# Stick-breaking attention: the last key's values are added in branch A's staging on GpSimd instead of in the eviction

## The chip, the cores and the metric

One core of a Trainium2 chip runs the whole layer. The metric is the device time of one execution in microseconds. TensorE (PE) multiplies, VectorE (DVE) and ScalarE (ACT) work on tiles in SBUF and read TensorE's results from PSUM banks, GpSimd (POOL) works on SBUF alone, SyncE (SP) issues most DMAs. Each engine runs its own instructions in a fixed order and waits for others on semaphores.

## The reference

One layer of an encoder, 1024 tokens by 1024 channels, in float32. The part that matters here is attention and the projection behind it:

```python
for i in range(s_len // Q_BLOCK):                      # 8 blocks of 128 queries
    z = jnp.einsum('bhqd,bhkd->bhqk', qb, kp) * inv_sqrt
    mask = s_idx < t_idx
    log_not = jnp.where(mask, jax.nn.log_sigmoid(-z), 0.0)
    excl = lax.cumsum(log_not, axis=3, reverse=True) - log_not
    a = jnp.where(mask, jnp.exp(jax.nn.log_sigmoid(z) + excl), 0.0)
    outs.append(jnp.einsum('bhqk,bhkd->bhqd', a, vp))
...
y_b = cb * causal_dwconv(cc * cx, conv_w[l])
merged = (jax.nn.sigmoid(ga) * (y_a @ w_branch_a[l])
          + jax.nn.sigmoid(gb) * (y_b @ w_branch_b[l]))
```

There are 16 heads of 64 channels. Behind this follow an output projection, a residual sum and a SwiGLU feed-forward part.

## The kernel before

Every matrix product is done in three passes of rounded parts: a float32 operand is split into a high part (a copy on ACT) and a low part (a subtraction on DVE), and high x high, high x low and low x high are summed in PSUM.

**Attention's arithmetic.** The weights of a row of keys are differences of running products, so the kernel sums the running products against differences of neighbouring value rows, and adds one value row by itself: that of the last key that a block of 128 queries can see. These rows, turned so that channels lie on partitions, are the small tile `vlast`; before it is 64 channels x 16 heads x 8 blocks. `load_vlast` loads them in two halves of 8 heads, and `turn_vlast` turns them on PE with small transposes and copies them out.

**Steps.** `attention` is a generator that goes through 128 steps (16 heads x 8 query blocks i). A step issues the scores of its block (`att_scores`: matmuls into a bank `z`, a sigmoid on ACT into `pt`, a triangular mask on POOL, line 927), then the transposes of the block two steps back (`att_trans`: PE into a bank `tr`, split into the tiles `ath`/`atl` or `afh`/`afl` by ACT and DVE, lines 952 to 958), then its own running product (`att_scan`: a scan on DVE, line 937, and the odd columns on POOL, which appears under the helper's line 133 as `pt<-pt`). Bank `z` has two buffers, and five tiles `pt` go round.

**Values.** `att_av` multiplies four blocks of one head (g = 0 or 1: queries 0 to 511 or 512 to 1023) into the bank `o`, of which there is one. Partitions 0 to 63 and 64 to 127 of `o` hold two partial sums. The eviction follows: ACT copies the lower half to `oy` in four pieces of 128 columns, each with its block's column of `vlast` as a bias (line 975), DVE adds the upper half (line 977), and SP stores `oy` to `d_ya` (line 978). `att_av` yields after every second key block, and `attention` takes so many of these pieces at each step as its two small tables say. The next group cannot begin in `o` before DVE's addition has read it.

**Fillers.** Between attention's matmuls PE works on independent matmuls into the banks `pj`: the B section with the convolution, then branch B's projection (lines 1033 to 1035). Branch A's projection runs behind attention, and its first products stand already among the last fillers.

**Branch A's staging** (lines 1182 to 1188). For 16 pieces (two halves n of the tokens, eight pairs k of heads) SP loads `yr` from `d_ya`, ACT copies the high part and DVE subtracts for the low one, into tiles `ya` that take over attention's buffers. `yr` uses the four buffers of `ybh` and `ybl`, so a load waits for the split of the piece four before it. The first loads come before attention has ended, as soon as the buffers are free.

**Order.** Matmuls keep the order in which the code is written, and so do attention's instructions on DVE and POOL (lines 1131 to 1137). All else is placed by a scheduler that simulates the engines' timeline; what it decides is fixed when the program is built.

Of the kernel before, what the change touches and what calls it, by code (L numbers as in the profile page):

```python
# [9 lines left out]
F32 = mybir.dt.float32  # L10
F32R = mybir.dt.float32r
AF = mybir.ActivationFunctionType
ALU = mybir.AluOpType
# [4 lines left out]
P = 128  # L18
T = 1024
D = 1024  # L20
KT = D // P
H = 16
DH = 64
# [7 lines left out]
def block_kernel(tc, x, x_t, cols, ada_1, ada_2, ada_row, w_q, w_kv, w_cg, w_a, w_b, w_o, w_g, w_u, w_d, out):  # L31
    nc = tc.nc
# [7 lines left out]
    def nm(s):  # L40
        uid[0] += 1
        return f"{s}_{uid[0]}"
# [42 lines left out]
    ident = const.tile([P, P], F32, name="dm")  # L85
# [46 lines left out]
    def tt(eng, out, a, b, op):  # L132
        eng.tensor_tensor(out=out, in0=a, in1=b, op=op)  # L133
# [195 lines left out]
    for whole in (1, 1, 0, 0, 1, 1, 0, 1, 1, 1, 1):  # L329
        for e in range(2 - whole):  # L330
            r = slice(0, P) if whole else slice(64 * e, 64 * e + 64)
# [495 lines left out]
    bp = s3.enter_context(tc.tile_pool(name="phb", bufs=1, reuse_waits="tile"))  # L827
# [6 lines left out]
    def att_load(h):  # L834
        pr, e0 = h // 2, (h % 2) * DH
        sqt = bp.tile([P, T], F32R, tag="sq", bufs=2, name=nm("sqt"))
        skh = bp.tile([P, T], F32R, tag="skh", bufs=2, name=nm("skh"))
        skl = bp.tile([P, T], F32R, tag="skl", bufs=2, name=nm("skl"))
        for e in range(2):
            es = slice(e * DH, (e + 1) * DH)  # L840
            nc.sync.dma_start(sqt[es].bitcast(F32), d_q[e][pr, e0:e0 + DH, :])
            nc.sync.dma_start(skh[es].rearrange("p (i t) -> p i t", t=P).bitcast(F32), d_k[0][pr // 4][:, e0:e0 + DH, pr % 4].rearrange("i p t -> p i t"))
            nc.sync.dma_start(skl[es].rearrange("p (i t) -> p i t", t=P).bitcast(F32), d_k[1][pr // 4][:, e0:e0 + DH, pr % 4].rearrange("i p t -> p i t"))
        hd[h] = (sqt, skh, skl)

    def load_v(h, e):

        pr = h // 2
        d = d_v[h // 8][pr % 4]
        t_ = ("vb", "va")[e]  # L850
        vab[t_] = first_va if (h, e) == (0, 1) else v_tile(e)
        lastld[0] = nc.sync.dma_start(vab[t_], d[e:P + e])

    def att_dv(h, part):

        va, vb = vab["va"], vab["vb"]
        cs = slice(h % 2 * DH, h % 2 * DH + DH)
        dv = vb[:, :, cs]
        if part == 0:
            tt(nc.vector, dv, dv, va[:, :, cs], ALU.subtract)  # L860
            return
        vt = vts[h] = bp.tile([P, KT, P], F32R, tag="vt", bufs=2, name=nm("vt"))
        nc.scalar.activation(vt[:, :, :DH], dv, AF.Copy)
        tt(nc.vector, vt[:, :, DH:], dv, vt[:, :, :DH].bitcast(F32), ALU.subtract)

    def load_vlast(e):

        vl = bp.tile([9 - e, 512], F32, tag="vl", bufs=1, name=nm("vl")) if e else first_vl
        nc.sync.dma_start(vl[:8].rearrange("i (r d) -> i r d", d=P), d_v[e][:, P].rearrange("r i d -> i r d"))
        if e == 0:  # L870
            nc.sync.dma_start(vl[8:9], d_b)
        return vl

    def turn_vlast(e, vl):
        tr = pps.tile([P, 512], F32, tag="tr", bufs=NTR, name=nm("tr"))
        n = 9 - e
        for h in range(8):
            nc.tensor.transpose(tr[:DH, h * n:h * n + n], vl[:, h * DH:(h + 1) * DH], ident[:n, :n])
        o, t = vlast[:, 8 * e:8 * e + 8], tr[:DH, :8 * n].rearrange("p (h i) -> p h i", i=n)
        if e:  # L880
            nc.scalar.activation(o, t, AF.Copy)
        else:
            nc.scalar.activation(o, t[:, :, :8], AF.Copy)
            nc.vector.tensor_tensor(out=o, in0=o, in1=t[:, :, 8:9].broadcast_to([DH, 8, 8]), op=ALU.add)

    vlast = bp.tile([DH, H, 8], F32, name="vlast")
    hd, vts, vab = {}, {}, {}

    def at_tile(full):
# [43 lines left out]
    def att_scan(h, i):  # L933
        pt, off = ptof[h, i], D - (i + 1) * P
        first = pt[:, slice(D - 1, off, -2)]
        both = pt[:, slice(D - 2, off - 1 if off else None, -2)]
        nc.vector.tensor_tensor_scan(out=both, data0=first, data1=both, initial=1.0, op0=ALU.mult, op1=ALU.mult)  # L937
        mid = pt[:, slice(off + 1, D - 2, 2)]
        tt(nc.gpsimd, mid, mid, pt[:, slice(off + 2, D - 1, 2)], ALU.mult)
# [21 lines left out]
    def att_av(h, g):  # L961
        pr, e0 = h // 2, (h % 2) * DH
        vt = vts[h]
        o = pps.tile([P, 512], F32, tag="o", bufs=1, name=nm("o"))
        for j in range(4 * g + 4):
            full, d = j < 4 * g, j % 4
            c0 = 0 if full else d * P
            for e, t in enumerate(ats[h, g, full]):
                lastav[0] = nc.tensor.matmul(o[:, c0:], vt[:, j, :], t[:, 4 * d * P:4 * d * P + 512 - c0],  # L969
                                             start=(j + e == 0), stop=(j == 4 * g + 3 and e == 1))  # L970
            if j % 2 and j < 4 * g + 3:
                yield 0
        yv = bp.tile([DH, 512], F32, tag="oy", bufs=2, name=nm("oy"))
        for e in range(4):
            nc.scalar.activation(yv[:, e * P:(e + 1) * P], o[:DH, e * P:(e + 1) * P], AF.Identity,
                                 bias=vlast[:, h, 4 * g + e:4 * g + e + 1])
        nc.vector.tensor_tensor(out=yv, in0=o[DH:], in1=yv, op=ALU.add)
        nc.sync.dma_start(d_ya[g][e0:e0 + DH, pr, :], yv)
        yield 0
# [5 lines left out]
    def attention():  # L985

        av = []
        steps = [(h, i) for h in range(H) for i in (LAST if h == H - 1 else ORDER)]
        for s in range(len(steps) + DAV):
            flush[0] = s >= len(steps)  # L990
            if s < len(steps):
                h, i = steps[s]
                if s % 8 == (0 if h else 3) and h + 1 < H:
                    with tc.issue_after(lastld[0].ins):
                        att_load(h + 1)
                with tc.issue_after(lastz[0].ins) if s else ExitStack():
                    if s in (1, 2):
                        att_dv(0, s - 1)
                    if s % 8 in ((4, 6) if h % 2 else (3, 5)) and h + 1 < H:
                        att_dv(h + 1, s % 8 // 5)  # L1000
                    if s % 16 in (6, 7) and s + 16 < len(steps):
                        load_v(2 * (s // 16) + 2, 7 - s % 16)
                if s == 54:
                    with tc.issue_after(lastld[0].ins):
                        vl = load_vlast(1)
                if s == 56:
                    turn_vlast(1, vl)
                yield from att_scores(h, i)
            tr_ = att_trans(*steps[s - 2]) if 0 <= s - 2 < len(steps) else iter(())
            if s >= DAV and steps[s - DAV][1] % 4 == 3:  # L1010
                av[:] = [att_av(steps[s - DAV][0], steps[s - DAV][1] // 4)]
            yield from itertools.islice(tr_, 1)
            if s < len(steps):
                yield from (a_ for q in av[:1] for a_ in itertools.islice(q, (0, 0, 0, 0, 1, 0, 1, 0)[s % 8]))
            yield from tr_
            if s < len(steps):
                att_scan(*steps[s])
            for q in av[:1]:
                yield from itertools.islice(q, 9 if s >= len(steps) else (2, 0, 2, 0, 2, 0, 2 * (s > 8 * H - 8), 0)[s % 8])

    def ps_f():
        return pps.tile([P, 512], F32, tag="pj", bufs=NPJ, name=nm("pj"))
# [80 lines left out]
    with tc.high_priority():  # L1103
        att_load(0)
        for j in range(HEAD):
            next(fl)
            if j == 1:
                vl = load_vlast(0)
# [3 lines left out]
                for e in range(2):  # L1112
                    nc.sync.dma_start((hh, hl)[e][1][:, :4].bitcast(F32), d_h[e])
    at_ = attention()
    flush, nfl = [0], 0
    pe, mine = len(nc.cur_bb.bb.instructions), set()
# [64 lines left out]
    with tc.high_priority():  # L1181
        for j, (ya2, (n, k)) in enumerate(zip(ya_slots(), [(0, k) for k in range(7)] + [(1, 0), (1, 1), (1, 2), (0, 7)] + [(1, k) for k in range(3, 8)])):
            yr = fq.tile([P, 512], F32, tag=("ybh", "ybl")[j % 2], bufs=2, name=nm("yr"))
            nc.sync.dma_start(yr, d_ya[n][:, k, :])
            h_, l_ = ya2[:, 0], ya2[:, 1]
            nc.scalar.activation(h_, yr, AF.Copy)
            tt(nc.vector, l_, yr, h_.bitcast(F32), ALU.subtract)
            yah[n][k], yal[n][k] = h_, l_
# [141 lines left out]
    for ch in range(2):  # L1330
# [21 lines left out]
        for i in (0, 4, 1, 2, 3, 5, 6, 7) if ch else range(8):  # L1352
            n, t0 = i // 4, (i % 4) * P
# [37 lines left out]
            r = rstd_of(ss, 1.0 / D, dp, 1)  # L1391
# [412 lines left out]
```

## Time and profile before

| | |
|---|---|
| median of 3 runs | 1794.71 us (1792.99 to 1795.57) |
| profiled execution | 1793.84 us, of which the span 1791.8 us |
| granted TensorE clock | 1.00 in the whole span |
| PE busy | 1780.3 us, 99% of the span |
| ACT, DVE, POOL busy | 826.5, 1271.2, 342.1 us |
| attention | from about 597 us to 983 us of the span |
| branch A's staging, loads | first issue at 778.2 us, last at 986.0 us |

PE is the engine that sets the time. Matmuls are pipelined, so a matmul's length in the trace overlaps the next one's; time that PE loses shows in the distance between the starts of two of them. A 512-column matmul is followed by the next after 0.23 us.

### The profile page before, as it was taken

The page shows a single profiled execution, that of the slowest core. Times are in us where ns is not written, and L with a number is a line of the kernel's source. Part 1 is how long each engine was busy: PE and PEld are TensorE (multiplying, and loading weights), DVE is VectorE, ACT ScalarE, POOL GpSimd, SP SyncE. Part 2 cuts the span into 40 slices and gives each one's busy share as a digit, 9 for nine tenths or more (in the row PEclk, how much of TensorE's full clock was granted, in tenths as well). Part 3 has the DMA queues.
Part 4 walks back from the last instruction along what each step waited for, and adds up shares of the span by engine and source line. Part 5 has one row for each costly group of instructions (what it writes and reads, how often), then busy time and mean ns, then how long its engine had stood idle before and what let it go on. Part 6 is the DMA issues. An engine that isn't in the chain of part 4 may idle for free.

```text
span 1791.8 us, 24274 instructions
## 1 busy us (share of the span) xinstructions
PE 1780.3 (99%) x8355; PEld 1469.9 (82%) x8355; DVE 1271.2 (71%) x1998; ACT 826.5 (46%) x1555; POOL 342.1 (19%) x437
## 2 busy tenths in 40 slices
PE   9999999999999999999999999999999999999999
PEld 6888877888888788888888888888888888888887
DVE  6876487777874678777786764698867777643866
ACT  5534364333433567666675221764544444432320
POOL 0024334734231233333342100100000000000000
PEclk9999999999999999999999999999999999999999
DMA  9579655222634977797654866425534344399776
GB/s 375 168 244 384 238 190 165 76 92 93 230 133 147 295 190 200 209 326 196 162 140 167 286 210 208 129 95 170 207 130 149 145 186 158 138 343 331 262 232 219
DMA packets 162447, 359.05 MB, mean 200 GB/s; under 512 B 15026, under 2 KB 56330, under 8 KB 161172
## 3 DMA queue, kind: packets, MB, share of 16 engines
q1 hardware_dynamic: 125740, 289.65, 49.2%
q10 hardware_dynamic: 33096, 55.25, 8.7%
q0 software_dynamic: 3488, 12.59, 2.0%
q8 instruction: 67, 1.10, 0.2%
q14 instruction: 56, 0.46, 0.1%
HBM read 247.84 MB, written 109.62 MB: 200 GB/s over the span
## 4 chain that ended last, share of the span: by engine, by line
PE 91%; DMA 4%; DVE 2%; ACT 1%; issue 1%; POOL 1%; SPq 0%; POOLq 0%; DVEq 0%; ACTq 0%
PE e L128 8%; PE e L129 8%; PE e L127 8%; PE pj L127 7%; PE pj L128 7%; PE pj L129 7%; PE pj L294 7%; PE pj L1033 4%; PE pj L1035 4%; PE pj L1034 4%; PE o L969 3%; PE e L1631 3%; PE e L1633 3%; PE e L1632 3%; PE tr L952 3%; PE z L922 2%
## 5 line engine op out<-in xcount | busy, mean ns | idle before, releaser
L1247 ACT ACTIVATE whi<-raw 128x512 fp32r<-128x512 f32 x137 | 84.9, 628 | 159.4 <-PE e L128 101.9
L1248 DVE TENSOR_TENSOR wlo<-raw,whi 128x512 fp32r<-128x512 f32 x137 | 93.0, 686 | 67.6 <-ACT whi L1247 50.1
L133 POOL TENSOR_TENSOR pt<-pt 128x63 f32<-128x63 f32 (+7 forms) x128 | 97.8, 764 | 211.0 <-DVE pt L937 198.2
L128 PE MATMUL e<-big,whi 128*128 128x512 f32 x352 | 136.9, 389 | 0.0
L127 PE MATMUL e<-big,whi 128*128 128x512 f32 x352 | 136.5, 390 | 0.0
L129 PE MATMUL e<-big,wlo 128*128 128x512 f32 x352 | 136.1, 389 | 0.0
L294 PE MATMUL pj<-whi,big 128*128 128x512 f32 x448 | 132.9, 393 | 0.8 <-ACT big L263 0.5
L133 DVE TENSOR_TENSOR c<-pj,c 128x512 f32<-128x512 f32 x140 | 93.5, 683 | 52.9 <-PE pj L129 52.3
L924 ACT ACTIVATE pt<-z,rq 128x128 f32<-128x128 f32 (+1 forms) x192 | 107.3, 580 | 48.0 <-PE z L923 41.8
L127 PE MATMUL pj<-big,whi 128*128 128x512 f32 x320 | 124.9, 390 | 0.0
L129 PE MATMUL pj<-big,wlo 128*128 128x512 f32 x320 | 124.7, 390 | 0.0
L128 PE MATMUL pj<-big,whi 128*128 128x512 f32 x320 | 124.6, 389 | 0.0
L1632 PE MATMUL e<-wlo,f 128*128 128x512 f32 (+1 forms) x319 | 121.8, 382 | 0.0
L1631 PE MATMUL e<-whi,f 128*128 128x512 f32 (+1 forms) x319 | 121.6, 382 | 0.0
L1633 PE MATMUL e<-whi,f 128*128 128x512 f32 (+1 forms) x319 | 121.6, 382 | 0.0
L133 DVE TENSOR_TENSOR wlo<-raw,whi 128x512 fp32r<-128x512 f32 x108 | 91.6, 852 | 34.6 <-ACT whi L524 34.5
L524 ACT ACTIVATE whi<-raw 128x512 fp32r<-128x512 f32 x108 | 67.4, 630 | 99.6 <-PE pj L128 49.8
L1033 PE MATMUL pj<-big,whi 128*128 128x512 f32 x256 | 112.8, 440 | 0.0
L127 PE MATMUL e<-rh,whi 128*128 128x512 f32 x264 | 102.7, 389 | 0.0
L128 PE MATMUL e<-rl,whi 128*128 128x512 f32 x264 | 102.7, 389 | 0.0
L129 PE MATMUL e<-rh,wlo 128*128 128x512 f32 x264 | 102.0, 389 | 0.0
L937 DVE TENSOR_TENSOR_SCAN pt<-pt 128x64 f32<-128x64 f32 (+7 forms) x128 | 95.9, 749 | 8.2 <-POOL pt L927 7.6
(348 smaller groups left out, 4678.2 us busy)
## 6 DMA issues: line engine op xcount, KB each, us to landing
f<-d_f SPq DMA_DIRECT2D x77, 512.0 KB, 4.1
d_f<-fs SPq DMA_DIRECT2D x70, 512.0 KB, 2.6
raw<-w_cg SPq DMA_DIRECT2D x40, 512.0 KB, 3.9
raw<-w_u SPq DMA_DIRECT2D x26, 512.0 KB, 4.7
raw<-w_g SPq DMA_DIRECT2D x25, 512.0 KB, 3.4
raw<-w_kv SPq DMA_DIRECT2D x20, 512.0 KB, 5.2
ld<-ada SPq DMA_DIRECT2D x16, 512.0 KB, 9.3
d_t<-ts SPq DMA_DIRECT2D x16, 512.0 KB, 6.4
```

The costliest lines, as they stand in the source:

```text
L127: nc.tensor.matmul(ps, wh[:, k, :], fh[:, k, :], start=(k == 0 and not onto), stop=False, skip_group_check=onto)
L128: nc.tensor.matmul(ps, wh[:, k, :], fl[:, k, :], start=False, stop=False, skip_group_check=onto)
L129: last = nc.tensor.matmul(ps, wl[:, k, :], fh[:, k, :], start=False, stop=(k == 3), skip_group_check=onto)
L133: eng.tensor_tensor(out=out, in0=a, in1=b, op=op)
L294: nc.tensor.matmul(ps, a, b, start=(k == 0 and q == 0), stop=(k == KT - 1 and q == 2))
L924: nc.scalar.activation(pt[:, off + s0:off + s0 + m], z[:, :m], AF.Sigmoid, scale=rq[:, 1, i, h:h + 1])
L937: nc.vector.tensor_tensor_scan(out=both, data0=first, data1=both, initial=1.0, op0=ALU.mult, op1=ALU.mult)
L1033: nc.tensor.matmul(ps, wh, rh_, start=(k == 0), stop=False)
L1248: los.append(nc.vector.tensor_tensor(out=lo, in0=src, in1=hi.bitcast(F32), op=ALU.subtract))
L1631: nc.tensor.matmul(o, sh, w[0][:, c], start=(j == 0), stop=False)
L1632: nc.tensor.matmul(o, sh, w[1][:, c], start=False, stop=False)
L1633: nc.tensor.matmul(o, sl, w[0][:, c], start=False, stop=(j == NJ - 1))
```

## The change

The bias goes out of the eviction, which becomes one ACT copy of 512 columns and the same DVE addition. `vlast` becomes 128 partitions (both heads of a pair) x 8 pairs x 8 blocks, so the turning needs 4 transposes a half instead of 8. In the staging each `yr` gets one GpSimd addition: 128x512, with a column of `vlast` repeated over each block of 128 tokens. The eviction becomes a piece of its own in `att_av`, and the two tables in `attention` take the pieces in such a way that the matmuls stay where they were, while the eviction is written about a third of a step later.

```diff
@@ turn_vlast
-        for h in range(8):
-            nc.tensor.transpose(tr[:DH, h * n:h * n + n], vl[:, h * DH:(h + 1) * DH], ident[:n, :n])
+        for r in range(4):
+            nc.tensor.transpose(tr[:, r * n:r * n + n], vl[:, r * P:(r + 1) * P], ident[:n, :n])
...
-    vlast = bp.tile([DH, H, 8], F32, name="vlast")
+    vlast = bp.tile([P, KT, 8], F32, name="vlast")
@@ att_av
-            if j % 2 and j < 4 * g + 3:
+            if j % 2:
                 yield 0
         yv = bp.tile([DH, 512], F32, tag="oy", bufs=2, name=nm("oy"))
-        for e in range(4):
-            nc.scalar.activation(yv[:, e * P:(e + 1) * P], o[:DH, e * P:(e + 1) * P], AF.Identity,
-                                 bias=vlast[:, h, 4 * g + e:4 * g + e + 1])
+        nc.scalar.activation(yv, o[:DH], AF.Copy)
         nc.vector.tensor_tensor(out=yv, in0=o[DH:], in1=yv, op=ALU.add)
@@ attention
-                yield from (a_ for q in av[:1] for a_ in itertools.islice(q, (0, 0, 0, 0, 1, 0, 1, 0)[s % 8]))
+                yield from (a_ for q in av[:1] for a_ in itertools.islice(q, (0, 1, 0, 0, 1, 1, 1, 0)[s % 8]))
...
-                yield from itertools.islice(q, 9 if s >= len(steps) else (2, 0, 2, 0, 2, 0, 2 * (s > 8 * H - 8), 0)[s % 8])
+                yield from itertools.islice(q, 9 if s >= len(steps) else (1, 0, 2, 0, 1, 0, 9 * (s > 8 * H - 8), 0)[s % 8])
@@ staging
             nc.sync.dma_start(yr, d_ya[n][:, k, :])
+            yb = yr.rearrange("p (i t) -> p i t", t=P)
+            tt(nc.gpsimd, yb, yb, vlast[:, k, 4 * n:4 * n + 4].unsqueeze(2).broadcast_to([P, 4, P]), ALU.add)
             h_, l_ = ya2[:, 0], ya2[:, 1]
```

On ACT, this is what stands around the eviction of head 9's second half, in step 4 of head 10 (the numbers behind the names count tiles and differ between the two programs). Before:

```order
L957 ACTIVATE ath_8176<-tr_8241 128x3x128
L863 ACTIVATE vt_8264<-vb_7766 128x8x64
L975 ACTIVATE oy_8257<-o_8184,vlast 64x128 x4
L924 ACTIVATE pt_5128<-z_8267,rq 128x256
L924 ACTIVATE pt_5128<-z_8274,rq 128x512
```

And after:

```order
L957 ACTIVATE ath_8111<-tr_8176 128x3x128
L974 ACTIVATE oy_8216<-o_8119 64x512
L863 ACTIVATE vt_8192<-vb_7710 128x8x64
L924 ACTIVATE pt_5128<-z_8195,rq 128x256
L924 ACTIVATE pt_5128<-z_8202,rq 128x512
```

The four pieces are one, and the value tile's copy (`vt`) has gone behind it; the sigmoids (`pt`) still follow both.

On DVE, at the eviction of head 8's first half in step 0 of head 9 (a scan is printed as SCALAR_TENSOR_TENSOR; `mb` is a filler's product, `afl` and `atl` are low parts of transposed products). Before:

```order
L937 SCALAR_TENSOR_TENSOR pt_5130<-pt_5130 128x64
L977 TENSOR_TENSOR oy_7857<-o_7753,oy_7857 64x512
L1083 TENSOR_TENSOR mb_7884<-pj_7789,sgi_7559 128x512
L958 TENSOR_TENSOR afl_7739<-tr_7874,afh_7738 128x4x128
L958 TENSOR_TENSOR atl_7759<-tr_7887,ath_7758 128x4x128
```

And after:

```order
L937 SCALAR_TENSOR_TENSOR pt_5130<-pt_5130 128x64
L1081 TENSOR_TENSOR mb_7821<-pj_7733,sgi_7502 128x512
L958 TENSOR_TENSOR afl_7683<-tr_7811,afh_7682 128x4x128
L975 TENSOR_TENSOR oy_7824<-o_7697,oy_7824 64x512
L958 TENSOR_TENSOR atl_7703<-tr_7828,ath_7702 128x4x128
```

The addition that frees the bank `o` now stands behind a split of the next block, here behind a filler's product as well.

On POOL, in the last steps of head 14 (`pt ... 128x511` is the running product of block 7; `yr` are the new additions):

```order
 L927 AFFINE_SELECT pt_5131<-pt_5131 128x128
+L133 TENSOR_TENSOR yr_9828<-yr_9828,vlast 128x512
 L133 TENSOR_TENSOR pt_5131<-pt_5131 128x447
 L927 AFFINE_SELECT pt_5127<-pt_5127 128x128
+L133 TENSOR_TENSOR yr_9834<-yr_9834,vlast 128x512
+L133 TENSOR_TENSOR yr_9846<-yr_9846,vlast 128x512
+L133 TENSOR_TENSOR yr_9840<-yr_9840,vlast 128x512
 L133 TENSOR_TENSOR pt_5127<-pt_5127 128x511
 L927 AFFINE_SELECT pt_5128<-pt_5128 128x128
```

Four additions stand ahead of attention's products of blocks 6 and 7. Head 15 has one ahead of its block 5 (128x383) and three ahead of its block 7; four stand in the steps of heads 8 and 9, one ahead of head 14's block 4, and the other three behind attention's last product.

More of the change, by code (lines that the diff above doesn't have):

```diff
@@ L876, in turn_vlast @@
         n = 9 - e
-        for h in range(8):
-            nc.tensor.transpose(tr[:DH, h * n:h * n + n], vl[:, h * DH:(h + 1) * DH], ident[:n, :n])
-        o, t = vlast[:, 8 * e:8 * e + 8], tr[:DH, :8 * n].rearrange("p (h i) -> p h i", i=n)
+        for r in range(4):
+            nc.tensor.transpose(tr[:, r * n:r * n + n], vl[:, r * P:(r + 1) * P], ident[:n, :n])
+        o, t = vlast[:, 4 * e:4 * e + 4], tr[:, :4 * n].rearrange("p (r i) -> p r i", i=n)
         if e:
@@ L883, in turn_vlast @@
             nc.scalar.activation(o, t[:, :, :8], AF.Copy)
-            nc.vector.tensor_tensor(out=o, in0=o, in1=t[:, :, 8:9].broadcast_to([DH, 8, 8]), op=ALU.add)
-    vlast = bp.tile([DH, H, 8], F32, name="vlast")
+            nc.vector.tensor_tensor(out=o, in0=o, in1=t[:, :, 8:9].broadcast_to([P, 4, 8]), op=ALU.add)
+    vlast = bp.tile([P, KT, 8], F32, name="vlast")
     hd, vts, vab = {}, {}, {}
```

## Prediction

> **What bounds the kernel.** I read the page first, then the busy times by stretches over attention, then the waits inside it, then the timeline of each engine at the places that the change touches.
>
> ```profile
> span 1791.8 us, 24274 instructions
> PE 1780.3 (99%) x8355; PEld 1469.9 (82%) x8355; DVE 1271.2 (71%) x1998; ACT 826.5 (46%) x1555; POOL 342.1 (19%) x437
> PE 91%; DMA 4%; DVE 2%; ACT 1%; issue 1%; POOL 1%; SPq 0%; POOLq 0%; DVEq 0%; ACTq 0%
> ...
> 205.00:597.00 392.00, 392.00 (x1734) 320.91 (x1732) 278.13 (x401) 155.94 (x259) 138.61 (x93) 1.00 0.44 148
> 597.00:700.00 103.00, 101.96 (x566) 84.30 (x566) 82.24 (x135) 72.58 (x165) 41.55 (x75) 1.00 0.78 216
> 700.00:800.00 100.00, 99.75 (x566) 84.13 (x565) 78.64 (x127) 69.92 (x158) 39.80 (x70) 1.00 0.89 269
> 800.00:900.00 100.00, 99.39 (x551) 82.75 (x551) 73.23 (x122) 65.81 (x153) 35.14 (x70) 1.00 0.72 185
> 900.00:985.00 85.00, 83.54 (x443) 69.34 (x442) 62.66 (x98) 54.88 (x121) 26.20 (x45) 1.00 0.50 154
> ```
>
> A row of stretches gives the length, then busy time of PE, weight loads, DVE, ACT and POOL, the granted clock and DMA. PE is busy 99% and makes up 91% of the chain; over attention it is idle 1.04 + 0.25 + 0.61 + 1.46 = 3.4 us of 388. ACT is at 70% there and DVE near 77%, so work taken from them is worth only what PE waits for them. What PE waits for:
>
> ```profile
> DVE oy L977 <- ACT oy L975: 12.8, 22, 1.0
> PE tr L952 <- POOL pt L133: 2.0, 5, 0.9
> PE z L922 <- ACT pt L924: 1.2, 6, 0.2
> ```
>
> (us in total, times, longest.) DVE idles 12.8 us for the eviction's four copies, but PE's own waits name only the sigmoid on ACT, six times, and POOL's running product, five times. The change touches both: it shortens what stands ahead of the sigmoid, and it puts work ahead of the product.
>
> **The shorter eviction.** One of the six waits, in step 4 of head 10, and the last of them, on ACT and PE:
>
> ```profile
> 832.33 0.63 ACT L863 ACTIVATE vt<-vb 128x512 fp32r<-128x512 f32 x1 [0.43 <-PE o L969]
> 832.87 1.11 ACT L975 ACTIVATE oy<-o,vlast 64x128 f32<-64x128 f32 x4
> 833.87 0.47 ACT L924 ACTIVATE pt<-z,rq 128x256 f32<-128x256 f32 x1
> ...
> 833.78 0.40 PE L1035 MATMUL pj<-big,wlo 128*128 128x512 f32 x1
> 834.39 0.44 PE L922 MATMUL z<-skh,sqt 128*128 128x384 f32 x1 [0.21 <-ACT pt L924]
> ...
> 950.02 0.40 PE L1035 MATMUL pj<-big,wlo 128*128 128x512 f32 x1
> 950.61 0.44 PE L922 MATMUL z<-skh,sqt 128*128 128x384 f32 x1 [0.19 <-ACT pt L924]
> ...
> L1518 ACT ACTIVATE c<-e 128x512 f32<-128x512 f32 x20 | 11.6, 582 | 0.0
> ```
>
> The starts are 0.61 us apart where 0.23 is normal: 0.38 lost, six times, 2.3 us. The four copies hold ACT from 832.87 to 833.87, 1.00 us. One copy of 512 columns out of PSUM takes 0.58 (last row), of which the next instruction overlaps 0.1, as `vt` shows (0.63 long, the next 0.54 after its start). So the sigmoid comes 0.5 us sooner, more than 0.38: these waits go, **-2.3 us** (bounds: -1.0 if other ACT work moves in, and -2.9 with some of POOL's 2.0 us of waits gone too, because DVE no longer idles 12.8 us). What is late next is nothing: PE's next matmul was ready.
>
> **The turning of vlast.** Eight transposes hold PE from 597.02 to 597.37:
>
> ```profile
> 597.02 0.42 PE L878 MATMUL tr<-dm,vl 9*64 9x9 f32 x8
> 597.37 0.50 PE L1033 MATMUL pj<-big,whi 128*128 128x512 f32 x1
> ```
>
> Four instead of eight, in two halves: 2 x 0.17, **-0.3 us**.
>
> **The later eviction.** Bank `o` is single, so the next group waits for DVE's addition, which now stands behind a split. At the end of head 8's first half:
>
> ```profile
> 801.13 0.69 DVE L977 TENSOR_TENSOR oy<-o,oy 64x512 f32<-64x512 f32 x1 [0.29 <-ACT oy L975]
> 802.09 0.69 DVE L1083 TENSOR_TENSOR mb<-pj,sgi 128x512 f32<-128x512 f32 x1 [0.27 <-PE pj L1035]
> 802.70 0.68 DVE L958 TENSOR_TENSOR afl<-tr,afh 128x512 fp32r<-128x512 f32 x1
> ...
> 803.40 0.48 PE L969 MATMUL o<-afh,vt 128*128 128x512 f32 x1
> ```
>
> The filler's product at 802.09 waits for PE itself and comes no sooner; the split follows to 803.38, and the addition then ends 0.61 later, at 803.99, where PE wants the bank at 803.40: 0.59 lost. In the new order a filler's instruction stands ahead of split and addition in this way at three handovers (heads 7, 8, 12). Elsewhere the split moves up by the 0.29 to 0.98 us that DVE no longer waits. I take 3 x 0.4, **+1.2 us** (bounds 0 and 3).
>
> **GpSimd's additions.** The nearest rows are the 128x512 additions of the gates, on POOL, with the DVE subtraction beside them (min/median/max ns):
>
> ```profile
> L133 POOL TENSOR_TENSOR ws<-raw x20: 1280/1736/1777, 175.9 to 556.6; 128x512 f32<-128x512 f32 x20
> L755 POOL TENSOR_TENSOR ws<-raw,ws x20: 1292/1613/1774, 178.9 to 559.7; 128x512 f32<-128x512 f32 x20
> L133 DVE TENSOR_TENSOR wlo<-ws,whi x80: 669/682/1775, 199.0 to 567.6; 128x512 fp32r<-128x512 f32 x80
> ```
>
> So 1.29 us alone and up to 1.78 beside DVE, 16 times, 21 to 28 us in all on an engine that is busy 31% of the last stretch. Nothing of it need reach PE, but POOL runs in order, and an addition that waits for its load holds back the running product behind it. Worst is head 14, where three stand ahead of block 7's product:
>
> ```profile
> 932.50 2.72 DVE L133 TENSOR_TENSOR ya<-yr,ya 128x512 fp32r<-128x512 f32 x3 [0.21 <-ACT ya L1186]
> 933.95 1.62 SPq L1184 DMA_DIRECT2D yr<-d_ya  x3
> DMA to landing us min/median/max: 2.9/3.0/3.4
> 936.67 1.21 DVE L937 TENSOR_TENSOR_SCAN pt<-pt 128x512 f32<-128x512 f32 x1
> ...
> 938.02 1.33 POOL L133 TENSOR_TENSOR pt<-pt 128x511 f32<-128x511 f32 x1 [3.95 <-DVE pt L937]
> ...
> 939.41 0.44 PE L952 MATMUL tr<-dm,pt 128*128 128x128 f32 x2 [0.87 <-POOL pt L133]
> ```
>
> The three loads leave as DVE's splits free their buffers, from 933.95, and land from 936.95. Three additions of 1.29 behind one another end at 940.8, the product 1.33 later at 942.15 instead of 939.35. PE has no cover here: it already waits 0.87 us for this product. So +2.8 clean, +4.2 with a collision of 0.46 each (1.75 less 1.29). I take **+3.3**, nearer the clean rows, since the loads also leave up to 0.5 sooner (bounds +1.5 and +5.6, below).
>
> In head 15 the same three stand ahead of its block 7:
>
> ```profile
> 960.20 1.27 SPq L1184 DMA_DIRECT2D yr<-d_ya  x3
> 964.16 1.05 POOL L133 TENSOR_TENSOR pt<-pt 128x511 f32<-128x511 f32 x1 [6.10 <-DVE pt L937]
> ...
> 968.41 0.39 PE L952 MATMUL tr<-dm,pt 128*128 128x128 f32 x2
> ```
>
> Two of the additions take their data from these loads, which land from 963.2; they end at 965.8, and the product ends at 966.9, ahead of 968.41: fillers cover it, with 1.5 us to spare. The rest have cover of that kind too (attention's products are used two steps later); I put **+0.3** on all of them (bounds 0 and 2). The last addition, behind attention, lies on the path from the last load:
>
> ```profile
> 991.08 0.63 ACT L1186 ACTIVATE ya<-yr 128x512 fp32r<-128x512 f32 x1 [5.31 <-DMA yr<-d_ya]
> 993.49 0.69 DVE L133 TENSOR_TENSOR ya<-yr,ya 128x512 fp32r<-128x512 f32 x1
> ```
>
> ACT's copy moves from 991.1 to 992.4 and ends at 993.0, before DVE comes to the low part at 993.49: nothing.
>
> **Sum.** -2.3 - 0.3 + 1.2 + 3.3 + 0.3 = +2.2 us on the profiled execution's 1793.84, so 1796.0. The runs' median is 0.87 above that execution; I put the forecast between the two bases, at **1796.5**, 0.1% over the median of before.
>
> **A rule against the change.** The rows above show a subtraction of 0.68 us that once took 1.78, 1.09 longer, and additions longer by 0.46. The Trainium skill, page "SBUF — State Buffer", section "SBUF: two separate sides", says why: GpSimd shares a port pair with VectorE under an exclusive lock, and against a VectorE instruction with two SBUF inputs the loser waits for the whole of the other. The trace agrees in size. By that rule alone the 16 additions could hold DVE for 16 x 1.29 = 20.6 us, and if all of it reached PE, 1793.84 - 2.6 + 20.6 would be 1811.8, as an estimate. But in the gates (205 to 597) 80 such additions ran beside DVE, and PE was busy 392.00 of 392 us. So a blocked DVE costs only where PE waits for it, which is the second rival.
>
> **Rivals.** (1) *The additions are hidden after all.* DVE's 12.8 us less of idling could bring the three splits, and so the loads, 2.8 us forward. Against it: the splits at 932.50 wait for ACT and a scan, not for the eviction. Without the 3.3 and half of the 1.2 the time is 1793.84 - 2.3 - 0.3 + 0.6 + 0.3 = 1792.1.
>
> (2) *Slower: additions and splits block each other at the end of head 14.* One addition (the fourth of head 14) runs as the three splits do. If each split waits for a POOL instruction, 0.46 to 1.09 longer each, the loads leave some 1.8 us later and the scan at 936.67 too; the product ends near 945.0 and PE loses 5.6 instead of 3.3. Head 15 then overdraws its 1.5 us by about as much again: 1796.0 + 2.3 + 1.5 = 1799.8. It decides once the loads land later than 938.5. For it: the first of the three splits already took much of its group's 2.72 us, where three alone take 3 x 0.68.
>
> (3) *The sigmoid's waits stay*, because `vt` or staging copies take the freed time on ACT: 1796.0 + 2.3 = 1798.3.
>
> **Chances.** Forecast 0.50, rivals 0.17, 0.23, 0.10. The measurement can tell about 0.2%, 3.6 us, from no change: below 1791.1 or above 1798.3. Faster takes the lower tail of the first rival: 0.07. Slower takes most of the second, half of the third and a tail of the forecast: 0.28. The rest is 0.65. The range 1791.5 to 1801.5 takes in both ends of the additions' cost and leaves a tenth outside on each side.
>
> **What the profile after would show.** The six waits of PE's scores for the sigmoid gone, and `oy` one copy near 0.58 us; PE's transposes of head 14's block 7 waiting 3 to 5 us for POOL, behind three `yr` additions of 1.3 to 1.8; waits of `o` for DVE's `oy` at two or three handovers; PE in 985 to 1065 unchanged. Wrong it would be if the product's place in head 14 has no growing wait, or if waits for `o` come at most handovers.

## The result, and the profile after

The changed kernel takes 1803.55 us (median of 4 runs, 1802.16 to 1804.11), the one before 1794.16 beside it: 1.0051 times as long, 95% interval 1.0033 to 1.0068. It is slower by 9.4 us; the forecast was +2.2, and the range ended at 1801.5. The profiled execution took 1803.08 us with a span of 1800.5. The page of the changed kernel, the first two of its rows:

```profile
span 1800.5 us, 24185 instructions
...
PE 1782.8 (99%) x8347; PEld 1471.4 (82%) x8347; DVE 1275.4 (71%) x1998; ACT 811.4 (45%) x1459; POOL 363.2 (20%) x453
```

ACT has 15 us less to do and POOL 21 us more, as meant. The stretches over attention, in the columns used for before:

```profile
597.00:700.00 103.00, 99.79 (x548) 82.44 (x547) 80.81 (x133) 67.39 (x137) 40.85 (x75) 1.00 0.77 212
700.00:800.00 100.00, 97.47 (x540) 80.86 (x539) 78.10 (x125) 65.31 (x131) 38.93 (x69) 1.00 0.87 266
800.00:900.00 100.00, 99.35 (x555) 83.37 (x554) 74.63 (x119) 61.70 (x125) 39.10 (x72) 1.00 0.70 179
900.00:985.00 85.00, 81.03 (x426) 66.89 (x424) 62.38 (x96) 46.90 (x95) 41.64 (x60) 0.98 0.47 130
```

PE is idle 3.2 + 2.5 + 0.65 + 4.0 = 10.4 us where it was 3.4, and in the last stretch the granted clock is 0.98. So the loss is not only in the last stretch, where it was looked for. The waits of the same kernel between 597 and 1000 us (us in total, times, longest):

```profile
DVE pt L937 <- POOL pt L927: 15.5, 26, 3.2
...
POOL yr L133 <- DMA yr<-d_ya: 11.1, 5, 3.0
...
PE tr L952 <- POOL pt L133: 7.1, 9, 3.4
```

Four places carry it, all from the timeline of the changed kernel (start, length, engine, line, tiles; what ended the wait). **Head 8, the first addition:**

```profile
780.87 0.32 SPq L1182 DMA_DIRECT2D yr<-d_ya  x1
...
789.75 1.04 POOL L133 TENSOR_TENSOR yr<-yr,vlast 128x512 f32<-128x512 f32 x1 [2.99 <-DMA yr<-d_ya]
790.74 0.29 POOL L927 TENSOR_SCALAR_AFFINE_SELECT pt<-pt 128x128 f32<-128x128 f32 x1
...
791.06 0.69 DVE L937 TENSOR_TENSOR_SCAN pt<-pt 128x256 f32<-128x256 f32 x1 [3.16 <-POOL pt L927]
...
791.84 0.61 POOL L133 TENSOR_TENSOR pt<-pt 128x255 f32<-128x255 f32 x1 [0.81 <-DVE pt L937]
...
792.51 0.66 PE L952 MATMUL tr<-dm,pt 128*128 128x128 f32 x4 [1.78 <-POOL pt L133]
```

The load leaves at 780.87 and its addition starts 8.9 us later, after GpSimd has stood idle for 2.99 us. Behind the addition stands the mask, behind that DVE's scan, then the product and PE's transposes. PE loses 1.95 us. **Head 14, block 7:**

```profile
938.00 3.11 SPq L1182 DMA_DIRECT2D yr<-d_ya  x3
...
940.89 1.04 POOL L133 TENSOR_TENSOR yr<-yr,vlast 128x512 f32<-128x512 f32 x1
...
942.22 1.21 DVE L937 TENSOR_TENSOR_SCAN pt<-pt 128x512 f32<-128x512 f32 x1
...
942.32 3.38 POOL L133 TENSOR_TENSOR yr<-yr,vlast 128x512 f32<-128x512 f32 x2 [0.40 <-DVE atl L958]
...
943.35 1.46 DVE L133 TENSOR_TENSOR wlo<-raw,whi 128x512 fp32r<-128x512 f32 x1
...
945.66 1.03 POOL L133 TENSOR_TENSOR pt<-pt 128x511 f32<-128x511 f32 x1
...
946.75 1.12 PE L952 MATMUL tr<-dm,pt 128*128 128x128 f32 x4 [3.39 <-POOL pt L133]
947.52 0.78 PE L1031 MATMUL pj<-big,whi 128*128 128x512 f32 x1
948.10 0.63 PE L1032 MATMUL pj<-big,whi 128*128 128x512 f32 x1
```

PE loses 3.55 us here (1.04 before). This stall is of another kind than the one at head 8: GpSimd idles only 0.40 us between the three additions, and it is their own length that holds the product back. The two at 942.32 take 3.38 us, 1.30 more than two of 1.04, while a subtraction on DVE beside them takes 1.46 us instead of 0.68. Then PE's matmuls start 0.42 to 0.58 us apart instead of 0.23, until 949.7: 1.3 us more. The stretch around it shows the granted clock (third number from the end):

```profile
945.00:950.00 5.00, 3.25 (x13) 2.81 (x14) 2.55 (x5) 0.64 (x2) 2.48 (x5) 0.66 0.34 114
```

**Head 2, a weight's copy on ACT that now stands ahead of two sigmoids,** and **head 8, bank `o`:**

```profile
659.07 0.63 ACT L524 ACTIVATE whi<-raw 128x512 fp32r<-128x512 f32 x1 [3.42 <-DMA raw<-w_cg]
659.60 1.25 ACT L924 ACTIVATE pt<-z,rq 128x512 f32<-128x512 f32 x2
...
660.33 0.33 PE L922 MATMUL z<-skh,sqt 128*128 128x128 f32 x1 [2.08 <-ACT pt L924]
...
807.18 0.69 DVE L1081 TENSOR_TENSOR mb<-pj,sgi 128x512 f32<-128x512 f32 x1 [1.25 <-PE pj L1033]
807.78 0.68 DVE L958 TENSOR_TENSOR afl<-tr,afh 128x512 fp32r<-128x512 f32 x1
808.50 0.69 DVE L975 TENSOR_TENSOR oy<-o,oy 64x512 f32<-64x512 f32 x1
...
809.34 0.47 PE L969 MATMUL o<-afh,vt 128*128 128x512 f32 x1 [0.61 <-ACT pt L924]
```

PE loses 2.24 us at the first and 0.77 at the second. There the wait ends with DVE's addition (808.50 + 0.69 = 809.19); ScalarE, which the row names, was not the last. The six waits for the sigmoid in heads 9 to 14 are gone.

### The profile page after: what moved, and what is told of

It is laid out like the page before. It is cut to its first block, busy times and chain, and to the rows that moved or that the text cites. A ratio compares the mean times of both kernels' runs of the same rounds, so it can differ in the third digit from the quotient of the medians.

```text
span 1800.5 us, 24185 instructions
## 1 busy us (share of the span) xinstructions
PE 1782.8 (99%) x8347; PEld 1471.4 (82%) x8347; DVE 1275.4 (71%) x1998; ACT 811.4 (45%) x1459; POOL 363.2 (20%) x453
## 4 chain that ended last, share of the span: by engine, by line
PE 93%; DVE 2%; POOL 1%; DMA 1%; issue 1%; ACT 1%; SPq 0%; POOLq 0%; ACTq 0%; DVEq 0%
PE pj L294 8%; PE e L128 8%; PE e L129 8%; PE e L127 8%; PE pj L127 7%; PE pj L129 7%; PE pj L128 7%; PE pj L1031 4%; PE pj L1033 4%; PE pj L1032 4%; PE e L1631 4%; PE e L1633 4%; PE e L1632 4%; PE o L969 3%; PE tr L952 3%; PE e L1368 2%
## 5 line engine op out<-in xcount | busy, mean ns | idle before, releaser
L952 PE MATMUL tr<-dm,pt 128*128 128x128 f32 x576 | 95.9, 276 | 7.3 <-POOL pt L133 7.1
```

What stands on the lines that cost most here:

```text
L952: nc.tensor.transpose(tr[:, j * P:(j + 1) * P], pt[:, off + (b0 + j) * P:off + (b0 + j + 1) * P], ident)
```

## The experiments: the two halves apart

The theory after this: the short eviction brings what was forecast, its later place costs more than forecast, and the additions cost by what they keep waiting behind them in GpSimd's queue. Four kernels separate the eviction (four copies or one, old or later place) from the additions. The two without additions leave the last keys' values out of the sum.

**One copy in its later place, no additions.**

```diff
-            tt(nc.gpsimd, yb, yb, vlast[:, k, 4 * n:4 * n + 4].unsqueeze(2)..., ALU.add)
```

> The changed kernel without GpSimd's 16 additions in the staging (so the last keys' values are left out of the sum): the one-copy eviction in its later place alone. Theory: the additions cost 6.3 us, the stalls of PE that lead back to GpSimd in the changed kernel's trace (1.95 at 790 us, 2.5 more than before at 943, 1.3 of slower matmuls behind that, 0.55 at 966); the eviction's reordering keeps the wait of 2.1 us at 657 and the wait of 0.6 us for bank o at 808. Then 1803.5 - 6.3 = 1797.2 us, slower than the kernel before by 3. Rival: all of the loss comes from the additions, and the eviction brings its 2.6 us: 1791.6.

**One copy in the old place, no additions** (also the old condition and tables):

```diff
-            if j % 2:
+            if j % 2 and j < 4 * g + 3:
```

> One copy of 512 columns as eviction, but written where the eviction stood before (the old condition and both old tables), and no additions on GpSimd (the last keys' values are left out of the sum). Theory: six waits of the scores for the sigmoid and half of vlast's turning go, and nothing else is reordered: 1794.2 - 2.2 - 0.3 = 1791.7 us; no wait at 657, none for bank o at 808. Rival: the wait at 657 belongs to the short copy, which lets the scheduler put the weight's split forward, not to the place: then 1793.8 and the wait is there.

**Additions alone** (on the kernel before, of zeros):

```diff
+            tt(nc.gpsimd, yb, yb, vzero[:, k, 4 * n:4 * n + 4].unsqueeze(2)..., ALU.add)
```

> The kernel before with its four copies and the bias, and GpSimd's 16 additions in the staging, of a tile of zeros as large as the new vlast: the additions alone. Theory: 1794.2 + 6.3 = 1800.5 us, with PE waiting for GpSimd's running product near 790 us (about 2) and at the end of head 14 (about 3.5, where it waited 1.0). Rival: the eviction's new place costs nothing and the additions carry the whole loss and the gain that is lost in it: 1794.2 + 9.4 + 2.5 = 1806.

**One copy in the old place, with additions** (the changed kernel with the line and tables of the second one):

> The changed kernel, with all of its arithmetic, but with the one-copy eviction written where it stood before (the old condition and both old tables). Theory: 1791.7 + 6.3 = 1798.0 us: the stalls for GpSimd stay, those at 657 and 808 go. Rival: the later place helps the end of attention (GpSimd's order there differs from the changed kernel's at two places), and the time is that of the changed kernel, 1803.5, within 1.

Medians in us, with the ratio to the kernel before (1793.32 beside these four) and its interval:

| eviction | without additions | with 16 additions |
|---|---|---|
| four copies, old place | 1793.32 | 1802.86, 1.0054 (1.0041 to 1.0066) |
| one copy, old place | 1789.36, 0.9978 (0.9969 to 0.9987) | 1800.83, 1.0042 (1.0029 to 1.0055) |
| one copy, later place | 1795.32, 1.0010 (1.0001 to 1.0019) | 1803.55 (the change, from its own set) |

The one copy brings 4.0 us, its later place takes 6.0 back, and the additions cost 8.2 to 11.5. In the profiles, from the first turning of `vlast` to the first matmul behind branch A, the kernels without additions take 467.1 us (before), 464.1 (old place) and 469.0 (later place), so there the copy brings 3.0 and the place costs 4.9. The additions were thought at 6.3, and cost more in every row. In the kernel with additions alone they stop PE at the same two places, for 3.69 and 3.56 us, each time with a slow clock behind it (waits from 597 to 1012 us, then the stretch after the first; the profile is of the longest of its five runs):

```profile
PE tr L954 <- POOL pt L133: 8.4, 5, 3.5
```

```profile
790.00:795.00 5.00, 4.16 (x13) 3.58 (x14) 4.28 (x7) 1.40 (x3) 3.83 (x5) 0.50 1.03 395
```

## The experiments: what the later place costs

**VectorE's addition ahead of the split** (later eviction, no additions on GpSimd; the tables' mid pieces are the old ones):

```diff
+            if s < len(steps) and s % 4 == 1:
+                for q in av[:1]:
+                    yield from itertools.islice(q, 1)
             yield from itertools.islice(tr_, 1)
```

> The changed kernel without the additions (the last keys' values are left out), with the eviction written after the next step's scores but ahead of its first split, so that VectorE's addition that frees bank o stands ahead of that split instead of behind it; ScalarE's weight copy near 657 us stays ahead of the two sigmoids, and TensorE's order is the same. Theory: the addition's place behind the split is what makes PE wait for bank o (0.29, 0.27, 0.21 and 0.77 us at 620, 668, 784 and 807 in the kernel without additions): 1795.3 - 1.5 = 1793.8 us, with the wait at 657 still there. Rival: the lateness of ScalarE's copy, not the split, makes bank o late, since the copy too is written later: 1795.3 and the four waits stay.

1790.07 us, 0.9981 (0.9972 to 0.9989): 5.3 of the 6.0 come back. The waits without additions, later place first, then this kernel:

```profile
PE tr L952 <- POOL pt L133: 3.0, 5, 1.3
PE z L922 <- ACT pt L924: 2.1, 1, 2.1
PE o L969 <- ACT pt L924: 0.6, 1, 0.6
```

```profile
PE tr L952 <- POOL pt L133: 2.3, 3, 1.1
PE z L922 <- ACT pt L924: 1.2, 1, 1.2
```

TensorE's and GpSimd's orders are the same in both, and ScalarE's copies of `o` keep their places, though they too are written earlier. On DVE 30 of the 32 additions stand earlier; besides them one scan, two other copies on ACT and eleven DMA issues moved. So the place of DVE's addition is what costs. Its price was more than bank `o` (1.25 us at three handovers in the first of these profiles): with the bank's waits went two waits for POOL's product (0.36 and 0.39 at 685 and 777 us) and half of the one for the sigmoid, where the weight's load now lands 6.2 us after its issue instead of 7.1. The expectation, 3.7 us too high, had counted the bank alone.

**The weight's copy behind the two sigmoids again** (later place, no additions):

```diff
+                    with tc.issue_after(sigs[2, 7].ins) if m == 4 else ExitStack():
+                        a_ = g_split(raw[:, :512])
```

> The one-copy eviction in its later place without the additions (the last keys' values are left out), and one instruction moved on ScalarE: the copy of a weight's high part near 657 us stands behind the two sigmoids of head 2's last block again, as in the kernel before. Theory: PE's wait of 2.1 us there was the weight's load, for which ScalarE stood still with the sigmoids behind it; 1795.3 - 2.2 = 1793.1 us, and no wait for the sigmoid at 657. Rival: the sigmoids would wait there for something else (or the weight is then late for its product): 1795.3, with a wait of another name.

1794.19 us, 1.0006 (0.9997 to 1.0015), 1.1 under the kernel without this instead of 2.2. The wait has another name now. ACT, then the wait behind it:

```profile
659.62 0.63 ACT L524 ACTIVATE whi<-raw 128x512 fp32r<-128x512 f32 x1 [2.84 <-DMA raw<-w_cg]
```

```profile
PE tr L953 <- DVE afl L959: 1.0, 1, 1.0
```

The load still lands at 659.6. The sigmoids no longer wait for it, but the split of PE's transposes, behind it in ACT's queue, does. The theory and its rival were each half right.

## The experiments: why the additions cost

**The additions behind the products** (one copy, old place, full arithmetic):

```diff
+            hi_ = ((8, 3), (8, 4), (8, 7), (9, 0), (14, 4), (14, 6), (14, 7), (14, 7), (14, 7), (15, 5))[j] if j < 10 else (15, 7)
+            with tc.issue_after(prods[hi_].ins):
                 tt(nc.gpsimd, yb, yb, ...)
```

> The full arithmetic, the eviction as one copy in its old place, and GpSimd's additions each ordered behind the running product ahead of which the scheduler had put it (three of head 14 and those of head 15 behind the products of block 7, the first two behind the products of blocks 3 and 4 of head 8). Theory: an addition costs by what it keeps waiting behind it on GpSimd, so the stalls of PE near 787 (2.1 and 0.7) and 939 (3.6, of which 1.0 was there without additions) and the slower matmuls behind the second (2.9) go: 1800.8 - 8 = 1792.5 us, less if the later staging makes branch A wait. Rival: the additions cost by taking VectorE's port from it, wherever they stand: 1799 or more.

1796.33 us, 1.0013 (1.0004 to 1.0021): 4.5 us better than with the additions ahead of the products, where 8 were expected. Its times lie apart (1792.86 to 1797.33; the seven longest have a mean granted clock of 0.998 to 0.999), and the profile is of one at 1792.91. In that one PE's waits for GpSimd are near those of the kernel before, 2.9 us in six against 2.0 in five: POOL at the end of head 14, then the waits.

```profile
934.95 1.34 POOL L940 TENSOR_TENSOR pt<-pt 128x511 f32<-128x511 f32 x1 [1.91 <-DVE pt L938]
936.25 0.29 POOL L928 TENSOR_SCALAR_AFFINE_SELECT pt<-pt 128x128 f32<-128x128 f32 x1
936.51 3.03 POOL L133 TENSOR_TENSOR yr<-yr,vlast 128x512 f32<-128x512 f32 x3
```

```profile
PE tr L953 <- POOL pt L940: 2.9, 6, 1.0
```

The three additions behind the product take 3.03 us together, 1.01 each. What the longer runs lose is not shown.

**ScalarE instead of GpSimd** (the piece in place, four copies with the bias):

```diff
+            for e in range(4):
+                nc.scalar.activation(yr[:, e * P:e * P + P], yr[...], AF.Identity, bias=vlast[:, k, 4 * n + e:4 * n + e + 1])
```

> The full arithmetic, one-copy eviction in its old place, and the last keys' values added to the staging's piece in place by ScalarE (four copies of 128 columns with the bias) instead of GpSimd. Theory (it is GpSimd's queue, not the added time on the piece's way, that cost 11 us): ScalarE's sigmoids cover it, 1789.4 + 1 = 1790.5 us. Rival: the piece's way from load to split is what matters, since the later loads wait for it and VectorE for the copy: at least half of the 11 us stays, 1795 or more.

1798.41 us, 1.0029 (1.0019 to 1.0039): the rival's time came. ACT and PE at the first load:

```profile
785.52 1.28 ACT L1184 ACTIVATE yr<-yr,vlast 128x128 f32<-128x128 f32 x4 [2.66 <-DMA yr<-d_ya]
...
787.37 0.39 PE L922 MATMUL z<-skh,sqt 128*128 128x256 f32 x1 [2.15 <-ACT pt L924]
```

So it is not GpSimd's queue alone: ScalarE, too, stops attention when it reads this load early with attention's work behind it. PE loses 2.31 us there, and then 1.1 to 1.6 us at three places from 928 to 943 us, of which only the first was followed: ScalarE waits there 1.05 us for another load. In the kernel before nothing reads the load of head 8 early. Its first reader is the split, which also needs a tile that attention still holds, and starts at 921 us.

**The sum inside the split** (no pass more: ACT's copy takes the bias, DVE makes (yr + bias) - high, in blocks of 128):

```diff
+                nc.scalar.activation(h_[:, c], yr[:, c], AF.Identity, bias=b)
+                nc.vector.scalar_tensor_tensor(out=l_[:, c], in0=yr[:, c], scalar=b, in1=h_[:, c]..., op0=ALU.add, op1=ALU.subtract)
```

> The full arithmetic without GpSimd's additions and without a pass more: one-copy eviction in its old place, and in the staging the high part is made on ScalarE by four copies of 128 columns with the bias, the low part on VectorE by four operations (yr + bias) - high. Theory: nothing stands ahead of the running products, ScalarE and VectorE have the room: 1789.4 + 0.5 = 1790 us, faster than the kernel before by 3. Rival: four short instructions instead of one on VectorE (16 times, some 0.5 us longer each) push the scans of heads 14 and 15 back, where PE waits for them: 1792 to 1794.

1796.89 us, 1.0021 (1.0012 to 1.003), 7 us above the expectation and 3 above its rival's upper end. In the profile (of the shortest run, 1794.24) four short DVE instructions take 1.13 to 1.23 us where one took 0.68, and attention's splits stand behind them. DVE, then the waits:

```profile
958.31 1.13 DVE L1187 SCALAR_TENSOR_TENSOR ya<-yr,vlast,ya 128x128 fp32r<-128x128 f32 x4
959.68 1.23 DVE L1187 SCALAR_TENSOR_TENSOR ya<-yr,vlast,ya 128x128 fp32r<-128x128 f32 x4 [0.25 <-ACT ya L1186]
```

```profile
PE tr L952 <- DVE afl L958: 3.5, 2, 2.1
```

**GpSimd adds at the eviction, before the store** (one copy, old place, `vlast` as before):

```diff
         nc.vector.tensor_tensor(out=yv, in0=o[DH:], in1=yv, op=ALU.add)
+        tt(nc.gpsimd, yb, yb, vlast[:, h, 4 * g:4 * g + 4].unsqueeze(2).broadcast_to([DH, 4, P]), ALU.add)
         nc.sync.dma_start(d_ya[g][e0:e0 + DH, pr, :], yv)
```

> The full arithmetic with vlast as in the kernel before, the one-copy eviction in its old place, and GpSimd adding the last keys' values to each eviction's result (64x512, 32 times instead of 16) before it is stored; nothing is added in the staging. Theory: an addition on GpSimd costs where it waits for a load with the running products behind it; here its data lies ready within a microsecond, and products are used two steps later, so 32 additions of 1.0 us cost less than the 16 of the staging did: 1789.4 + 2 = 1791.5 us, under the kernel before. Rival: GpSimd's time itself is what costs (33 us more on it, beside VectorE's scans): 1789.4 + 11 or more, over 1800.

**1789.95 us, 0.9983 (0.9974 to 0.9992): the full arithmetic, faster than both kernels.** There are 32 additions as long as the staging's shortest, 33 us more on POOL in all. They cost 0.6 us over the kernel without any (medians of two sets; 1.2 in the profiles, over the stretch used above). The tile's instructions (ns, shortest/median/longest), then the waits:

```profile
L133 POOL TENSOR_TENSOR oy<-oy,vlast x32: 1032/1036/1485, 620.8 to 978.6; 64x512 f32<-64x512 f32 x32
```

```profile
PE tr L952 <- POOL pt L133: 3.5, 7, 1.0
```

So GpSimd's time cost next to nothing at these places. The operand lies ready here, behind the product of the same step; no addition waits for a load, and no three stand in a row ahead of a product. Which of the two counts for how much was not separated.

**Additions for the last four pieces only** (the kernel before, with one copy and additions for the second halves of heads 8 to 15, behind the last product), and then the same with the new small tile padded:

```diff
+        if late_add(g, pr):          # g == 1 and pr >= 4
+            nc.scalar.activation(yv, o[:DH], AF.Copy)
...
-    vpair = bp.tile([P, 4, 8], F32, name="vpair")
+    vpair = bp.tile([P, 8, 8], F32, name="vpair")
```

> The kernel before, but for the second halves of heads 8 to 15 the eviction is one copy, and GpSimd adds their last keys' values in the staging of these four pieces, behind attention's last running product; the other evictions keep the four copies with the bias, all in the old place. vlast of these heads is turned once more by four small transposes. Theory: the six waits of the scores for the sigmoid lie in these evictions and go (-2.2), and four additions behind the last product delay no product: 1793.0 - 2.2 + 0.3 = 1791 us. Rival: the last piece's way (load, addition, split) now ends attention later: 1793 or more.

> The kernel before with four pieces' additions behind attention (as the run named hybrid), and the small tile of turned values made 256 bytes long on each partition instead of 128; every instruction stands where it stood. In the run without this, attention was 2.0 us shorter than before, and behind it the 362 matmuls of branch A followed one another at 232 to 233 ns instead of 227, 2.0 us longer in all. Theory: tiles behind the small one lay 128 bytes off, and the pace is that of the operands' addresses; with 256 bytes it is 227 again and the time 1794.5 - 2.0 = 1792.5 us. Rival: the pace has to do with what the additions or loads do beside it: 232 stays, and 1794.5.

1794.47 us, 1.0006 (0.9997 to 1.0015), and padded 1791.51, 0.9989 (0.998 to 0.9998), better by 3.0 where 2.0 were expected. The first is as long as its rival said, but not for the rival's reason: in both the six waits are gone and attention is shorter by 1.6 to 2.0 us than before, and without the padding branch A's matmuls, 2.0 us longer in all, gave that back. Its matmuls from 985 to 1060 us (busy and mean ns), first unpadded, then padded:

```profile
L1045 PE MATMUL pj<-ya,whi 128*128 128x512 f32 x63 | 24.9, 396 | 0.3 <-DVE sgi L1226 0.3
```

```profile
L1045 PE MATMUL pj<-ya,whi 128*128 128x512 f32 x63 | 24.6, 391 | 0.3 <-DVE sgi L1226 0.3
```

## Why the prediction was wrong, by its steps

- **The shorter eviction, -2.3: right in its mechanism, somewhat small.** All six waits went, and with the place unchanged the profile shows -3.0, the medians -4.0. Where the rest comes from was not followed. (ACT's share over attention was 68%, not the 70% read; nothing hangs on it.)
- **The turning, -0.3: wrong by its size.** PE's next matmul comes 0.34 us after the start of four transposes (596.24 to 596.58 in the changed kernel) as against 0.35 for eight: 0.0.
- **The later eviction, +1.2: the term that was mis-sized most, 4.9 in the profile.** Three handovers were counted, and only bank `o`. The changed kernel shows four with a loss of 0.2 to 0.8, 1.5 in all, and the runs show more beside them: a late addition on DVE delays what stands behind it there and on POOL, and the order of ACT and SP moves too. The copy of the weight ahead of two sigmoids was visible in ACT's new order and was not priced; it cost 2.2 at 657 us.
- **Head 14, +3.3: nearly right as a wait** (3.55 where it was 1.04, so +2.5) and wrong in what follows: behind the wait TensorE's clock was lower, +1.3 more. That price was in no term. An addition alone took 1.04 and not 1.29 us, and the collisions with DVE made up for it.
- **"The rest have cover", +0.3: the step whose reasoning failed; it cost 2.9.** At head 8 PE lost 1.95 and then 0.41 us (3.69 with the additions alone), at head 15 0.55, behind an addition that waited 2.99 us for its load ahead of block 5; the three ahead of block 7 were covered, as forecast. The cover of two steps was held against an addition's length, and not against its load's flight of up to 8.9 us. A product is used two steps later, but the mask and the scan of the next step stand behind the addition too.
- **The last addition, nothing: right.** PE is busy 79.67 of 80 us from 985 to 1065 in both profiles.
- **The second rival** came nearer in time (1799.8), and its mechanism was there, but small: DVE and POOL did slow each other in head 14, by 1.30 us for two additions. It knew nothing of head 8 or of the eviction's place, so that it came nearer is in part luck. Nor do collisions cost by themselves: the 32 additions at the eviction, beside the same scans, cost about 1. The first rival fell. The third's six waits went, but one new wait for the sigmoid of 2.1 us came, behind the weight's copy, which it had not named.
- The sum by its steps from these profiles: -3.0 + 4.9 + 7.9 (the additions in the later place, 476.9 against 469.0 us in the stretch above) = +9.8, measured +9.4. Each step is the difference of two kernels in one chain, so the steps must add up; what PE lost at the places named makes some 6.3 of the 7.9, and the rest is not placed.

## What to carry to other kernels

Before giving work to an engine with room, look at what stands behind it in that engine's queue and when its operand lands: 16 additions that read a fresh load, up to three of them in a row, cost 8 to 11.5 us, and 32 whose operand lay ready, one at a time, cost about 1, on the same engine. When an addition frees a single bank, keep it ahead of the next block's work on its engine; one place later cost 5 us in all here. And price a reordering by every queue that it changes, the scheduler's side moves included, not by the edited instruction.

## What the runs showed of the hardware

**Long waits cost clock.** Behind PE's four waits of 3.39 to 3.52 us the granted clock fell to about half (0.50 in 790 to 795 us above) and the matmuls lost another 1.3 to 2.9 us. Five waits of 1.8 to 2.1 us left it at 1.00, but one of 2.15, with ScalarE's additions, was followed by slow matmuls 1.3 us after it. So the length of one wait does not decide alone. The stretches behind the longest of the five (2.14 us, the sum inside the split) and behind the one of 2.15:

```profile
962.00:968.00 6.00, 5.09 (x24) 4.29 (x25) 6.00 (x14) 3.52 (x10) 2.87 (x3) 1.00 0.64 196
```

```profile
787.00:793.00 6.00, 5.63 (x21) 4.64 (x22) 4.81 (x8) 5.78 (x15) 2.62 (x4) 0.72 1.04 390
```

The Trainium skill, page "TensorE: Matmul & The Clock Gate", part "Part 1: The HAM clock gate", says that the clock is halved after an idle window of about 3.4 us, in windows that run freely. The long waits agree with it in size and ratio; the one of 2.15 us is shorter than its window, and there the measurement decides.

**A tile's length in SBUF changed TensorE's pace.** With 128 bytes more on each partition, at the same order of instructions, the matmuls of branch A followed one another at 227 ns instead of 232; 227 is also the median in every other kernel here. Which operand's address does it was not tried.

**GpSimd's addition took 1.04 us** at its shortest for 512 columns, on 64 partitions as on 128, and in the changed kernel up to 1.93 beside VectorE. The 1.29 taken for "alone" in the prediction holds for the gates' additions: one at 483.05 us of the kernel before took 1.29 with VectorE busy for only 0.23 us of it. What makes the two kinds differ was not tried.
